# One paced sequence for the mixers of all four chunks, with the last two feed-forwards standing alone

## The chip, the cores and the metric

The kernel runs on one core of one Trainium2 chip. The metric is the device time of one execution in microseconds (us). The engines in the text are PE (TensorE: matrix products; PEld is its loading of the stationary operand), DVE (VectorE), ACT (ScalarE), POOL (GpSimd, which here issues DMAs) and SP (which issues DMAs too).

## The reference

One decoder block works on 2048 positions of width 1024, all in float32:

```
h   = rms_norm(x) * (1 + sc1) + sh1
proj = h @ w_in                       # 3088 columns: gq gk gv gr glr aq ak av
y_gla = gated linear attention, 4 heads, chunks of 64, state carried along the sequence
y_att = dilated attention, 8 heads, (window, dilation) = (128,1), (512,4), (2048,16), merged per position
x   = x + g1 * (concat(y_gla, y_att) @ w_out)
h   = rms_norm(x) * (1 + sc2) + sh2
u   = causal depthwise conv of width 3 over (h @ w_up)     # 2 x 2816 columns
x   = x + g2 * ((silu(u_gate) * u_val) @ w_down)
```

The six vectors sh1, sc1, g1, sh2, sc2, g2 come from one product of the condition with a weight of 1024 x 6144.

## The kernel before

The sequence is cut into four chunks of 512 positions (`NCH = 4`, `T = 512`). Each float32 product of weights is made of three passes in a rounded format (`mm3`, lines 306 to 308: high by high, high by low, low by high); a weight block arrives raw (L234), its high part is cut by ACT (L240) and its low part by DVE (L241). These products go to the four PSUM banks of the pool `psg`. The mixers use the four banks of the pool `psa`.

The generators of the program `yield` between steps, and `run` interleaves them:

- `gemm` is the projection of the four chunks with the late part of the condition product beside it: 100 steps of about 24 matmuls. `run` takes 27 of them ahead, so that 73 are left.
- `mix(c)` is the mixers of chunk `c`, 68 steps: two halves of linear attention (`gla`, 14 steps each: DVE lines 690 to 725 prepare and mask, PE L680 makes the scores, L739 to L779 the rest) and four pairs of attention heads (`attn`, 10 steps each: PE L865 and L830 make scores, DVE L836 adds the bias and takes the maximum, ACT L840 the exponentials, PE L897, L921 and L850 the merging factors and transposes, L949 and L954 the products with the values, L969 and DVE L972 the end).
- `outproj(c)` is the output projection, 8 steps, after which comes the second norm's statistic (PE L445, ACT L447 and L448), then a tail of work that was put off (4 or 8 steps), then the normalised input `h2` of the feed-forward (DVE L465, ACT L467, DVE L469).
- `ffn(c)` is the feed-forward: 44 up blocks of 24 matmuls (evacuated by ACT L1028, DVE L1029 to L1045) and five groups of 8 down steps of 12 matmuls (evacuated by DVE L1073); a sixth group is put off as the next chunk's tail.

`beside(a, na, b, nb)` takes `na / nb` steps of `a` after each step of `b`, and what is left of `a` at the end. Before, it is called four times: `mix(0)` beside the 73 steps of `gemm` (68/72, or 0.94 of a step each), and `mix(1)`, `mix(2)`, `mix(3)` beside `outproj(c-1)` and `ffn(c-1)` (96, 100 and 100 steps, at 68/90, 68/86 and 68/90: 0.76 to 0.79). `outproj(3)` and `ffn(3)` come last with nothing beside them.

```
def beside(a, na, b, nb):
    acc = 0.0
    done = object()
    for _ in b:
        acc += na / nb
        while acc >= 1.0:
            acc -= 1.0
            if next(a, done) is done:
                acc = -1e9
    for _ in a:
        pass
```

The order so written is the input of a scheduler that fixes each engine's order when the program is built; each engine then works through its own queue in order.

Of the kernel before, what the change touches and what calls it, by code (L numbers as in the profile page):

```python
# [21 lines left out]
NCH = 4  # L22
# [78 lines left out]
# [14 lines that stand above are left out]
def along(a, na, b, nb):  # L115
# [9 lines that stand above are left out]
        yield  # L125
    for _ in a:
        pass


def chain(*gs):  # L130
    for g in gs:
        yield from g


class K:
# [945 lines left out]
    def run(self):  # L1081
        self.ada_setup()
        self.scratch()
        self.x1, self.h2, self.tail = {}, {}, ()
        self.planned = False
        xs = self.load_x(0)
        acc = None
        for k in range(5):
            acc = self.square(acc, xs[k])
        sqs = [self.tmp.tile([P, T], F32, name="sq", bufs=3) for _ in range(5, KD)]  # L1090
        for sq, x in zip(sqs, xs[5:]):
            self.nc.scalar.activation(sq, x, AF.Square)
        rstd = {0: self.norm_end(acc, more=sqs)}
        h0, ws, done = [], {}, {b: self.pg() for b in FIRST}
        spare = self.at.tile([P, 2048], F32R, name="w0", tag="kt", bufs=2)
        ring = self.at.tile([P, 2048], F32, name="ring", tag="kt", bufs=2)
        for k in range(KD):
            big = [self.at.tile([P, 1024], F32, name="wada", tag="big", bufs=4)]
            pair = [self.gp.tile([P, T], F32, name="wada", tag=t) for t in ("ghi", "glo")] if k < 5 else [ring[:, (k - 5) * 1024:(k - 4) * 1024] if k < 7 else self.at.tile([P, 1024], F32, name="wada", tag="v4", bufs=1)]
            gs = [self.ada(KD + k, big), self.ada(k, pair)]  # L1100
            for g in gs:
                next(g)
            if k < len(FIRST):
                b = FIRST[k]
                ws[b] = self.wblock(self.A["w_ch"][b], KD, P, spare if k == 3 else None)
            for g in gs:
                next(g, None)
            if k == GATE:
                self.gate_ins = self.last
            h0.append(self.norm_mod1(xs[k], k, rstd[0], self.G1, self.mod[:, 0:8]))  # L1110
        for b in FIRST:
            for k in range(KD):
                self.mm3(done[b], ws[b][k:k + 1], h0[k:k + 1], k == 0, True)
        self.consts()

        def src(c):
            def f(k):
                t = self.tmp.tile([P, T], F32, name="sq", bufs=3)
                ld = self.dq.dma_start(t, self.A["xT"][c, k])
                if c == 1:  # L1120
                    self.after(ld)
                return t
            return f

        self.wleft, self.wready, self.wpos = list(self.plan()), [], 0
        self.planned = True
        hs = [h0]

        def begin(c):
            hs.append(self.norm_mod(src(c), rstd[c], self.G1, self.mod[:, 0:8]))  # L1130

        def proj(c):
            yield from self.proj(c, hs.pop(), (lambda: begin(c + 1)) if c < 3 else None, () if c else done)

        def stats(c):

            acc = None
            xs = [src(c)(0)]
            yield
            for k in range(KD):  # L1140
                if k + 1 < KD:
                    xs.append(src(c)(k + 1))
                yield
                acc = self.square(acc, xs[k], xs[k])
            yield
            rstd[c] = self.norm_end(acc, split=True)
            yield

        def ahead(c):

            return along(stats(c), 11, proj(c - 1), 18)

        gemm = along(self.ada_late(), 66, chain(ahead(1), ahead(2), ahead(3), proj(3)), 94)
        for _ in range(27):
            next(gemm)
        beside(self.mix(0), 68, gemm, 72)
        beside(self.mix(1), 68, chain(self.outproj(0), self.ffn(0)), 90)
        beside(self.mix(2), 68, chain(self.outproj(1), self.ffn(1)), 86)
        beside(self.mix(3), 68, chain(self.outproj(2), self.ffn(2)), 90)
        for _ in chain(self.outproj(3), self.ffn(3)):  # L1160
            pass


# [59 lines left out]
```

## Time and profile before

| | |
|---|---|
| time | 2602.16 us, median of 2 runs (2600.97 and 2603.35) |
| profiled execution, first to last instruction | 2603.1 us, 46834 instructions |
| PE busy | 2559.7 us, 18142 matmul records |
| DVE busy | 1930.2 us |
| ACT busy | 1277.7 us |
| POOL busy | 444.4 us |
| mean granted TensorE clock | 0.994 |
| DMA | 405.13 MB, mean 156 GB/s |

The page gives the profiled execution no time of its own beside its span; the longer of the two runs is 0.25 us above that span. A matmul's record lasts until its modelled end, so records of one engine overlap: the rate of PE is read from the starts of its rows, not from its busy share. The stages of the span, by the first row of each: the projection with `mix(0)` from about 205 to 722 us, then three stretches from one feed-forward's first up block to the next, 1237.5, 1740.2 and 2237.2 us, and the last feed-forward alone from there to the end.

### The profile page before, as it was taken

Reading aid. Unit: us, or ns where it says so; the run is one execution under the profiler, and the core shown is the slowest. Engines: PE = TensorE matmul, PEld = TensorE weight load, DVE = VectorE, ACT = ScalarE, POOL = GpSimd, SP = SyncE. Lnnn points to the kernel's source line nnn. Section 1 sums busy time; section 2 is a strip of 40 time slices with the busy share of each in tenths; the row PEclk is TensorE's granted clock in tenths of the full one; section 3 lists DMA queues with packets and bytes.
Section 4 is the critical chain, followed back from the end, with each engine's and each line's share of the span. In section 5 each row is a group of like instructions: output and inputs, shape, how many; then the busy total and the mean of one; then the engine's idle time right before and its main releaser. Section 6 shows DMA issues by size and latency. Waiting matters only on the chain.

```text
span 2603.1 us, 46834 instructions
## 1 busy us (share of the span) xinstructions
PE 2559.7 (98%) x18142; PEld 2104.0 (81%) x18142; DVE 1930.2 (74%) x4091; ACT 1277.7 (49%) x2626; POOL 444.4 (17%) x816
## 2 busy tenths in 40 slices
PE   5999999999999999999999999999999999999999
PEld 4888888788788888887788888878888888788887
DVE  7578877768788777777987777689777775766665
ACT  4566556656454444454545544346445453433332
POOL 1343332313210000012100000310000003100001
PEclk8999999999999999999999999999999999999999
DMA  8766675756633344455334344733443435432322
GB/s 291 242 226 234 211 236 170 239 167 201 230 108 100 123 128 122 127 174 199 123 96 139 117 134 136 252 131 114 129 140 127 143 103 189 150 103 97 96 96 84
DMA packets 164194, 405.13 MB, mean 156 GB/s; under 512 B 19154, under 2 KB 61956, under 8 KB 162692
## 3 DMA queue, kind: packets, MB, share of 16 engines
q0 software_dynamic: 88128, 308.59, 35.5%
q1 hardware_dynamic: 75844, 93.55, 11.6%
q8 instruction: 143, 2.34, 0.4%
q14 instruction: 79, 0.65, 0.1%
HBM read 339.15 MB, written 62.91 MB: 154 GB/s over the span
## 4 chain that ended last, share of the span: by engine, by line
PE 77%; issue 1%; DVE 1%; DMA 1%; ACT 0%; POOL 0%; POOLq 0%; DVEq 0%; ACTq 0%
PE psg L306 22%; PE psg L307 22%; PE psg L308 22%; PE psa L850 2%; PE psa L830 2%; PE psa L954 2%; PE psa L680 1%; PE psa L949 1%; PE psa L865 0%; PE psa L753 0%; PE psa L752 0%; PE psa L969 0%; DMA wada<-in_w_ada_dram 0%; PE psa L757 0%; PE psa L779 0%
## 5 line engine op out<-in xcount | busy, mean ns | idle before, releaser
L306 PE MATMUL psg<-hhi,whi 128*128 128x512 f32 x1992 | 782.0, 396 | 9.2 <-ACT hhi L467 5.3
L307 PE MATMUL psg<-hlo,whi 128*128 128x512 f32 x1992 | 782.9, 394 | 6.7 <-DVE hlo L469 6.5
L308 PE MATMUL psg<-hhi,wlo 128*128 128x512 f32 x1992 | 780.2, 392 | 0.7 <-DVE wlo L241 0.7
L240 ACT CAST whi<-wraw 128x1024 fp32r<-128x1024 f32 (+1 forms) x391 | 410.4, 1051 | 467.4 <-PE psg L307 363.2
L241 DVE TENSOR_TENSOR wlo<-wraw,whi 128x1024 fp32r<-128x1024 f32 (+1 forms) x391 | 478.0, 1223 | 187.2 <-ACT whi L240 181.5
L306 PEld LDWEIGHTS psg<-hhi,whi 128*128 128x128 f32 x1992 | 375.0, 189 | 95.2 <-ACT hhi L467 9.3
L307 PEld LDWEIGHTS psg<-hlo,whi 128*128 128x128 f32 x1992 | 375.3, 188 | 86.7 <-DVE hlo L469 9.6
L308 PEld LDWEIGHTS psg<-hhi,wlo 128*128 128x128 f32 x1992 | 375.5, 188 | 80.6 <-issue 1.7
L306 PE MATMUL psg<-ghi,whi 128*128 128x512 f32 x744 | 295.1, 398 | 0.0
L307 PE MATMUL psg<-glo,whi 128*128 128x512 f32 x744 | 292.1, 393 | 0.5 <-DVE glo L999 0.5
L308 PE MATMUL psg<-ghi,wlo 128*128 128x512 f32 x744 | 291.6, 392 | 0.0
L234 POOL DMA_DIRECT2D wraw<-in_w_up_dram x176 | 93.6, 532 | 982.6 <-DVE wlo L241 850.5
L1073 DVE SCALAR_TENSOR_TENSOR x<-psg,mod,x 128x512 f32<-128x512 f32 x192 | 143.2, 749 | 118.2 <-PE psg L308 115.7
L306 PE MATMUL psg<-whi,hhi 128*128 128x512 f32 (+2 forms) x512 | 172.8, 345 | 8.3 <-ACT stg L523 6.2
L308 PE MATMUL psg<-whi,hlo 128*128 128x512 f32 (+2 forms) x512 | 174.8, 345 | 0.0
L307 PE MATMUL psg<-wlo,hhi 128*128 128x512 f32 (+2 forms) x512 | 174.6, 343 | 0.1
L306 PEld LDWEIGHTS psg<-ghi,whi 128*128 128x128 f32 x744 | 139.5, 188 | 34.0 <-issue 5.3
L307 PEld LDWEIGHTS psg<-glo,whi 128*128 128x128 f32 x744 | 139.8, 188 | 30.0 <-issue 1.9
L308 PEld LDWEIGHTS psg<-ghi,wlo 128*128 128x128 f32 x744 | 139.7, 188 | 29.5 <-issue 0.7
L840 ACT ACTIVATE big<-big,nm 128x256 f32<-128x256 f32 (+1 forms) x256 | 122.4, 480 | 33.6 <-DVE nm L855 33.4
L1028 ACT ACTIVATE y<-psg,tables_sb 128x512 f32<-128x512 f32 x176 | 136.1, 776 | 4.5 <-PE psg L308 3.2
L1029 DVE SCALAR_TENSOR_TENSOR y<-psg,tables_sb,y 128x511 f32<-128x511 f32 x176 | 130.7, 743 | 3.7 <-ACT y L1028 3.6
(253 smaller groups left out, 3621.9 us busy)
## 6 DMA issues: line engine op xcount, KB each, us to landing
wraw<-in_w_up_dram POOLq DMA_DIRECT2D x176, 512.0 KB, 3.6
wraw<-in_w_down_dram POOLq DMA_DIRECT2D x88, 512.0 KB, 3.6
wraw<-in_w_ch_dram POOLq DMA_DIRECT2D x44, 512.0 KB, 4.3
v<-v SPq DMA_DIRECT2D x68, 256.0 KB, 5.6
wada<-in_w_ada_dram POOLq DMA_DIRECT2D x64, 256.0 KB, 4.8
wraw<-in_w_tokw_dram POOLq DMA_DIRECT2D x32, 512.0 KB, 4.2
wraw<-in_w_out_dram POOLq DMA_DIRECT2D x32, 512.0 KB, 4.7
sq<-in_xT_dram POOLq DMA_DIRECT2D x48, 256.0 KB, 4.9
```

The costliest lines, as they stand in the source:

```text
L234: self.dq.dma_start(raw[:, :n], src)
L240: nc.scalar.copy(hi[:, :n], raw[:, :n])
L241: nc.vector.tensor_tensor(lo[:, :n], raw[:, :n], hi[:, :n].bitcast(F32), op=ALU.subtract)
L306: nc.tensor.matmul(ps, wh, hh, start=first and k == 0, stop=False, skip_group_check=shared)
L307: nc.tensor.matmul(ps, wh, hl, start=False, stop=False, skip_group_check=shared)
L308: self.lastmm = nc.tensor.matmul(ps, wl, hh, start=False, stop=k == n - 1, skip_group_check=shared)
L830: nc.tensor.matmul(at(i, hh, z), q[H[hh], i * P:(i + 1) * P], key(H[hh], i, z), start=True, stop=True, skip_group_check=True)
L840: nc.scalar.activation(t[:, lo:hi], t[:, lo:hi], AF.Exp, bias=nm[:, hh, g, i:i + 1], scale=2.0 ** -(h + 1), accum_out=dn[:, hh, g, i:i + 1])
L850: nc.tensor.transpose(ps[:n, i * P:(i + 1) * P], part(S[hh], i), self.C("id"))
L1028: nc.scalar.activation(y, ps, AF.Identity, bias=self.cb[:, b:b + 1], scale=self.cw[:, 2, b:b + 1])
L1029: nc.vector.scalar_tensor_tensor(y[:, 1:], ps[:, :T - 1], self.cw[:, 1, b:b + 1], y[:, 1:], op0=ALU.mult, op1=ALU.add)
L1073: nc.vector.scalar_tensor_tensor(x1, ps, self.mod[:, 40 + cb:41 + cb], x1, op0=ALU.mult, op1=ALU.add)
```

## The change

The four calls and the lone end become one call and a longer lone end. All 272 mixer steps run in one sequence, at 272/243 = 1.12 steps after each step of the chain `gemm`, `outproj(0)`, `ffn(0)`, `outproj(1)`, `ffn(1)` (73 + 96 + 100 = 269 steps). `outproj(2)`, `ffn(2)`, `outproj(3)`, `ffn(3)` then have nothing beside them. The order of the products of weights among themselves is the same, and so is the order of the mixers' steps among themselves; no instruction of either is added or removed.

```
-        beside(self.mix(0), 68, gemm, 72)
-        beside(self.mix(1), 68, chain(self.outproj(0), self.ffn(0)), 90)
-        beside(self.mix(2), 68, chain(self.outproj(1), self.ffn(1)), 86)
-        beside(self.mix(3), 68, chain(self.outproj(2), self.ffn(2)), 90)
-        for _ in chain(self.outproj(3), self.ffn(3)):
+        beside(chain(*(self.mix(c) for c in range(NCH))), 272, chain(gemm, self.outproj(0), self.ffn(0), self.outproj(1), self.ffn(1)), 243)
+        for _ in chain(self.outproj(2), self.ffn(2), self.outproj(3), self.ffn(3)):
             pass
```

On PE, this is the place behind `outproj(2)`, where the statistic of the norm (L445) is made and the put-off down steps of chunk 1 follow. Before:

```order
L307 MATMUL psg<-glo,whi 128x512
L308 MATMUL psg<-ghi,wlo 128x512
L445 MATMUL psa<-rstd,ones 128x512
L680 MATMUL psa<-pt 32x32 x64
L306 MATMUL psg<-ghi,whi 128x512
L307 MATMUL psg<-glo,whi 128x512
```

And PE at the same place in the changed kernel:

```order
L307 MATMUL psg<-glo,whi 128x512
L308 MATMUL psg<-ghi,wlo 128x512
L445 MATMUL psa<-rstd,ones 128x512
L306 MATMUL psg<-ghi,whi 128x512
L307 MATMUL psg<-glo,whi 128x512
```

The 64 score matmuls of `mix(3)` (L680) that stood there are gone to an earlier place: the last mixer matmul of the program (L969) stands behind 7851 of the 9792 `psg` matmuls before, and behind 5878 in the changed kernel.

On DVE, this is the start of the second half of linear attention of chunk 2 (`mix(2)`), with the work of the feed-forward around it. L663 to L704 are the mixers', L1029 to L1073 the feed-forward's, L241 the low part of a weight. Before:

```order
L183 COPY stage<-psa 128x512
L241 TENSOR_TENSOR wlo<-wraw,whi 128x1024
L663 COPY kt<-psa 128x512
L1041 SCALAR_TENSOR_TENSOR y_13467<-th,y_13467 128x512
L1029 SCALAR_TENSOR_TENSOR y_13558<-psg,tables_sb,y_13558 128x511
L1032 SCALAR_TENSOR_TENSOR y_13558<-halo,tables_sb,y_13558 128x1
L700 TENSOR_TENSOR pt<-kt 128x512
L1030 SCALAR_TENSOR_TENSOR y_13558<-psg,tables_sb,y_13558 128x510
L1045 TENSOR_TENSOR glo<-y_13467,ghi 128x512
L1033 SCALAR_TENSOR_TENSOR y_13558<-halo,tables_sb,y_13558 128x2
L1040 SCALAR_TENSOR_TENSOR th<-th,y_13513 128x512
```

And DVE at the same step of `mix(2)` in the changed kernel:

```order
L183 COPY stage<-psa 128x512
L663 COPY kt<-psa 128x512
L700 TENSOR_TENSOR pt<-kt 128x512
L1073 SCALAR_TENSOR_TENSOR x<-psg,mod,x 128x512
L241 TENSOR_TENSOR wlo<-wraw,whi 128x1024
L703 TENSOR_TENSOR pt<-kt,pt 128x512
L700 TENSOR_TENSOR pt<-kt 128x512
L704 TENSOR_TENSOR pt<-kt,pt 128x512
L1073 SCALAR_TENSOR_TENSOR x<-psg,mod,x 128x512
L703 TENSOR_TENSOR pt<-kt,pt 128x512
L700 TENSOR_TENSOR pt<-kt 128x512
L704 TENSOR_TENSOR pt<-kt,pt 128x512
```

The step stood among up blocks and now stands among down steps, and the rows of the mixers stand closer together: one or two operations for the feed-forward stand between three of theirs, where before three or four stood between two of theirs.

## Prediction

> **What bounds the kernel now.** I read the page first, then the table by stages, then PE's waits, then the starts of single matmuls.
>
> ```profile
> PE 2559.7 (98%) x18142; PEld 2104.0 (81%) x18142; DVE 1930.2 (74%) x4091; ACT 1277.7 (49%) x2626; POOL 444.4 (17%) x816
> PE   5999999999999999999999999999999999999999
> PE 77%; issue 1%; DVE 1%; DMA 1%; ACT 0%; POOL 0%; POOLq 0%; DVEq 0%; ACTq 0%
> ```
>
> PE is busy in every slice but the first, and the chain that ended last runs through PE for 77%, with 1% each for DVE and DMA. Since matmul records overlap, "busy" alone would hide small gaps; the starts settle it. In the last feed-forward, which has no mixer beside it:
>
> ```profile
> 2300.69 0.39 PE L307 MATMUL psg<-hlo,whi 128*128 128x512 f32 x1
> 2300.92 0.39 PE L308 MATMUL psg<-hhi,wlo 128*128 128x512 f32 x1
> ```
>
> One matmul of 512 columns per 0.23 us (0.227 over longer stretches). The stages, with the columns length, then busy time of PE, PEld, DVE, ACT and POOL, granted clock, DMA share, GB/s:
>
> ```profile
> 205.00:722.00 517.00, 512.26 (x4245) 428.23 (x4236) 398.08 (x918) 312.67 (x673) 158.20 (x282) 1.00 0.63 208
> 1237.50:1740.20 502.70, 498.61 (x3868) 407.20 (x3866) 387.31 (x892) 243.79 (x551) 60.54 (x113) 1.00 0.44 142
> 1740.20:2237.20 497.00, 494.69 (x3507) 403.75 (x3507) 372.27 (x855) 236.78 (x529) 60.97 (x114) 1.00 0.43 137
> 2190.00:2237.20 47.20, 44.99 (x195) 35.93 (x193) 28.40 (x36) 21.01 (x27) 9.12 (x17) 1.00 0.46 152
> 2237.20:2603.00 365.80, 361.17 (x1584) 298.25 (x1584) 236.80 (x369) 126.57 (x156) 38.98 (x73) 0.99 0.29 97
> ```
>
> A feed-forward alone takes 365.8 us, its output projection about 47.2: 413. With a mixer sequence beside it the period is 497, so a mixer sequence costs 84 us of PE time (497 less 413), in line and not hidden. The same subtraction on DVE: 372.3 less (236.8 + 28.4) is 107 us per sequence. PE has no room to give, so four sequences cost about four times 84 us wherever they stand. A reordering can only win or lose at the seams.
>
> **The change part by part.** No instruction is added or removed; 272 mixer steps move earlier. The sum is made against the profiled span of 2603.1 us, 0.9 above the median of the runs shown.
>
> *Seams between products of weights and mixers.* Each visit of PE to the mixers costs something at both ends:
>
> ```profile
> 1199.09 0.39 PE L308 MATMUL psg<-hhi,wlo 128*128 128x512 f32 x1
> 1199.41 0.29 PE L680 MATMUL psa<-kt 64*32 64x32 f32 x11
> ...
> 1199.91 0.50 PE L306 MATMUL psg<-hhi,whi 128*128 128x512 f32 x1
> 1200.25 0.40 PE L307 MATMUL psg<-hlo,whi 128*128 128x512 f32 x1
> ...
> 1009.13 0.39 PE L306 MATMUL psg<-ghi,whi 128*128 128x512 f32 x1
> 1009.36 0.60 PE L850 MATMUL psa<-consts_sb,big 128*128 128x128 f32 x4
> 1009.71 0.47 PE L307 MATMUL psg<-glo,whi 128*128 128x512 f32 x1
> 1010.02 0.39 PE L308 MATMUL psg<-ghi,wlo 128*128 128x512 f32 x1
> ```
>
> The last matmul before L680 holds PE 0.32 us (1199.09 to 1199.41) in place of 0.23, the first behind it 0.34: 0.2 us per visit. Around the transposes of L850 only the way out costs: 0.31 in place of 0.23, so 0.08. The built order has 334 visits before and 316 after, 18 fewer. At 0.15, between the two rows, that is **-2.7 us**; the ends are 18 times 0.08 and 18 times 0.2, or -1.4 and -3.6.
>
> *The boundary of chunk 2 loses its cover.* Behind an output projection PE works through the put-off steps and then waits for the normalised input. First with mixers beside it (chunk 2), then bare (chunk 3):
>
> ```profile
> 1738.13 0.39 PE L308 MATMUL psg<-ghi,wlo 128*128 128x512 f32 x1
> 1740.16 0.47 PE L306 MATMUL psg<-hhi,whi 128*128 128x512 f32 x1 [1.64 <-DVE x L1073]
> 1740.72 0.51 PE L307 MATMUL psg<-hlo,whi 128*128 128x512 f32 x1
> 1741.07 0.40 PE L308 MATMUL psg<-hhi,wlo 128*128 128x512 f32 x1
> ...
> 2235.33 0.39 PE L308 MATMUL psg<-ghi,wlo 128*128 128x512 f32 x1
> 2237.18 0.47 PE L306 MATMUL psg<-hhi,whi 128*128 128x512 f32 x1 [1.46 <-ACT hhi L467]
> 2237.75 0.50 PE L307 MATMUL psg<-hlo,whi 128*128 128x512 f32 x1
> ...
> 2239.28 0.63 PE L308 MATMUL psg<-hhi,wlo 128*128 128x512 f32 x1
> 2239.70 0.63 PE L306 MATMUL psg<-hhi,whi 128*128 128x512 f32 x1
> ```
>
> The covered boundary loses 2.03 less 0.23, 0.56 less 0.23 and 0.35 less 0.23: 2.3 us. The bare one loses 1.85 less 0.23 and 0.57 less 0.23, about 2.0 us, and then shows starts 0.42 us apart (2239.28 to 2239.70), which the covered one does not. Seven of those and a few smaller delays make up about 2 us more. One boundary changes from covered to bare: **+2 us**, between 0 (the wait itself is no longer than the covered one's) and +4 (the wait of 2.0 us comes twice).
>
> The Trainium skill, "TensorE: Matmul & The Clock Gate", Part 1 ("The HAM clock gate"), says that the array falls to half its clock after an idle window of about 3.4 us and comes back after a busy one as long. The doubled spacing here is such a clock, but the wait ahead of it was 1.46 us, under the window, and the covered boundary with 1.64 us kept its clock. By that rule the term would lose its clock part and be near 0; by the row it is +2.
>
> *The mixers' closer pace.* A step comes every 0.89 steps of the weights' products (243/272) in place of 1.06 beside the projection and 1.26 to 1.32 beside the feed-forwards. Whether PE then waits for the mixers' DVE and ACT work is the unknown. What PE waits for in `psa` now, the long wait at the start apart:
>
> ```profile
> PE psa L779 <- DVE pt L773: 0.9, 1, 0.9
> PE psa L680 <- DVE stage L972: 0.6, 1, 0.6
> PE psa L969 <- DVE pt L934: 0.3, 1, 0.3
> PE psa L662 <- DVE ll L657: 0.2, 1, 0.2
> ```
>
> That is 2.0 us in the whole span, though `mix(0)` already ran at 0.94 of a step. DVE's load: 82 of the 272 steps (73 times 1.12) now fall beside the projection, 190 (2.8 sequences) beside two feed-forwards. There PE has 2 times 413 plus 2.8 times 84, or 1061 us, and DVE 2 times 265 plus 2.8 times 107, or 830: 78%, against 75% in the row of chunk 2. Beside the projection DVE gets 398 plus 14 steps of 1.6 us (107/68), or 420 of 534 us: 79% against 77%. The cover is thin but there. The nearest row says 2 us of waits for 272 steps; a pace 1.2 to 1.5 times as close I value at **+3 us**. Bounds: -2 (those waits go) and +24, if each of the 12 pairs of heads beside the feed-forwards lost the 2.0 us that the worst four losses make up together.
>
> *The start of `outproj(0)`* no longer follows the end of `mix(0)` directly: that sequence ends at step 61 of 73, so its last stores are a dozen steps old when they are read back. The L680 wait of 0.6 us and the boundary's small ones may go: **-1 us**, 0 to -2. The end of the program (`outproj(3)` and `ffn(3)`) is as it was: 0.
>
> Sum: -2.7 + 2 + 3 - 1 = +1.3, or 2604.4 us; I say **2604**. The bounds add to 2595.5 (-3.6, 0, -2, -2) and 2629.7 (-1.4, +4, +24, 0).
>
> **The rivals.**
>
> *The chain inside a pair of heads becomes the bound; slower.* Ends of two pairs now:
>
> ```profile
> 1022.67 1.06 DVE L972 TENSOR_TENSOR stage<-psa,stage 128x512 f32<-128x512 f32 x1 [3.69 <-ACT stage L971]
> 1095.78 1.07 DVE L972 TENSOR_TENSOR stage<-psa,stage 128x512 f32<-128x512 f32 x1 [0.76 <-ACT stage L971]
> ```
>
> A pair took 73 us. Ten steps at the new pace are 8.9 steps of the feed-forward at 413/98 = 4.2 us and 10/68 of 84 us: 50 us. If scores, maxima, exponentials, merging factors and transposes need longer than that one after another, PE, which works in order, stands still at L897, L921 or L850 with products of weights queued behind it. It decides from 52/12 = 4.3 us per pair on, which is 2% of the time; at 6 us per pair the time is 2603 + 72 = 2675. For it: in the built order the fourth pair of chunk 2 ends some 100 `psg` matmuls (22 us) behind its pace, so the sequence is already held by its chain there. Against it: that delay was put into the order by moving mixers back, and PE fills it with products of weights; and at L897, L921 and L850, which already stand a few matmuls behind what they need, PE waits for nothing now.
>
> *DVE binds in the dense stretches of linear attention; a little slower.* In the rows of the change three mixer operations stand for each one or two of the feed-forward's. Six halves stand beside feed-forwards; if each holds PE up by 5 us, a quarter of a group of 8 down steps (22 us), the time is 2603 + 30 = 2633. Against it: the free banks of `psg` give 4 times 12 times 0.227, or 11 us of grace. The Trainium skill, "SBUF — State Buffer", section "Who interferes with whom", adds that VectorE in a two-port mode shuts GpSimd out, so that weights issued from POOL would come late too; no run here shows such a lock.
>
> *More than 2% faster.* All seams together are 316 visits that remain and at most 334 times 0.2, or 67 us, of which 18 go. To win 52 us, PE's waits inside the mixers would have to be large and hidden; the four rows above say 2 us. Time if every seam loss of the 18 visits and all waits above go: 2596.
>
> **Chances.** Forecast (2592 to 2618): 0.78. DVE in the dense stretches (2618 to 2655): 0.13. The chain of a pair (above 2655): 0.07. Much faster: 0.02. The range runs from 2592 to 2632, which holds a bit over 0.8. Faster by over 2% 0.02, within 2% 0.91, slower by over 2% 0.07; 2% is about what a measurement of this kernel can tell from no change.
>
> **What would show it.** The seams: PE's total of `psa` waits, and 0.3 us starts around L680, fewer by 18 pairs. The boundary: behind the third L445 after the start, starts 0.42 us apart as behind the fourth. The pace: PE's waits for L897, L921, L850 or L680, each a few us at most in sum; pairs of heads 50 us apart at L972; DVE near 78% from the first output projection to the end of the mixers, then 65%. The prediction is wrong if PE's busy slices fall to 9 tenths or less in the middle of the span, or if the stage with mixers ends later than four times 84 us of mixers allow.

## The result, and the profile after

The changed kernel takes **2634.27 us** (median of 2 runs, 2632.76 to 2635.78) against 2602.16: a ratio of 1.0124, with a 95% interval of 1.0094 to 1.0153. It is slower, and its median lies 2 us above the predicted range and 30 us above the predicted time; the interval, about 2627 to 2642 us, still reaches into the range. The profiled execution spans 2631.0 us, 27.9 us more than before.

The first lines of its page hardly differ from those of before. PE is as busy in every slice, and DVE has the same work; only its slices in the last third show that the mixers end earlier. What has changed is the chain that ended last: it now follows PE for 45% only, and the load of `kw` stands among its lines. (The listed shares add up to 47%, so this chain leaves half of the span untold, and the drop from 77% is no measure of lost time.)

```profile
PE 2573.8 (98%) x18142; PEld 2116.4 (80%) x18142; DVE 1933.7 (73%) x4091; ACT 1276.6 (49%) x2624; POOL 445.2 (17%) x816
PE   5999999999999999999999999999999999999999
DVE  7678977768787769877679877865766665766665
PE 45%; DVE 1%; DMA 1%; issue 0%; ACT 0%; SPq 0%; POOL 0%; POOLq 0%
```

The stages of the changed kernel (length, busy time of PE, PEld, DVE, ACT and POOL, clock, DMA share, GB/s): first the two stretches with mixers, from 722 us (in the output projection of chunk 0) to about the feed-forward of chunk 1 and from there to about that of chunk 2, then the two that stand alone.

```profile
722.00:1331.00 609.00, 605.24 (x5186) 489.66 (x5185) 472.12 (x1184) 315.98 (x796) 63.84 (x119) 1.00 0.44 143
1331.00:1852.00 521.00, 512.34 (x4041) 420.82 (x4039) 397.96 (x924) 250.30 (x570) 59.89 (x112) 0.99 0.42 139
1852.00:2263.00 411.00, 408.69 (x1796) 336.60 (x1795) 266.51 (x407) 160.87 (x239) 63.68 (x119) 1.00 0.36 123
2263.00:2631.00 368.00, 361.70 (x1587) 298.46 (x1585) 238.66 (x372) 128.54 (x159) 38.98 (x73) 0.99 0.29 98
```

DVE is at 472.12 of 609 and 397.96 of 521 us, 78% and 76%, and then at 65%: as forecast, and not the bound. PE's waits tell more (engine, tile and line, the one waited for: us in total, times, longest):

```profile
PE psg L306 <- ACT hhi L467: 12.6, 5, 4.4
PE psa L830 <- DMA kw<-k: 6.4, 8, 1.2
PE psa L865 <- DMA qf<-q: 2.9, 1, 2.9
PE psa L830 <- DVE md L836: 2.0, 2, 1.7
```

Waits for `kw`, `qf` and `md` are not in the list of before at all, and the wait for `hhi` is larger (12.6 against 5.3 us).

**Where the time went.** I took every time from one matmul's start to the next one's on PE and summed it by the line of the first. The sum grows by 28.2 us: 13.9 at the score matmuls L830 (65.2 to 79.1), 7.1 at L865, behind which the waits for `kw` stand (14.0 to 21.1), 4.2 in the products of weights, 2.6 at L501, 1.7 at L969, and 1.3 less in all others. Three places make most of it.

*The load of `kw`.* `kt`, `kw` and `v16` share two buffers, so the next pair's `kw` can only be loaded when L949 of this pair has read `v16`. Before, on PE and then on SP's queue:

```profile
1495.67 3.71 PE L954 MATMUL psa<-big,v 128*64 128x128 f32 x64
1518.34 1.13 PE L830 MATMUL psa<-kw,qf 64*128 64x256 f32 x8
...
1495.80 0.53 SPq L806 DMA_DIRECT2D kw<-k  x1
```

After:

```profile
902.08 3.71 PE L954 MATMUL psa<-big,v 128*64 128x128 f32 x64
906.31 0.86 PE L865 MATMUL psa<-kt,qf 64*32 64x64 f32 x64
908.14 1.10 PE L830 MATMUL psa<-kw,qf 64*128 64x256 f32 x4 [0.97 <-DMA kw<-k]
...
902.21 0.53 SPq L806 DMA_DIRECT2D kw<-k  x1
```

L954 starts when the last L949 has been issued, and the load follows 0.13 us later in both. Before, PE wants `kw` 22.5 us after that. After, it comes for `kw` within 6 us, and the load takes about 5.9 (902.21 to 908.14). From the last L949 of a pair to the first L830 of the next one, within a chunk, there were 13 to 29 us before (one of 5.0 in chunk 0, whose `kw` is smaller); after, eight of the twelve are 5.3 to 6.7 us.

*Scores of one head alone.* The scores of two heads use the two halves of the array. Before, eight records of both heads, and after, four records of one head:

```profile
1106.54 1.14 PE L830 MATMUL psa<-kw,qf 64*128 64x256 f32 x8
1107.60 0.50 PE L306 MATMUL psg<-ghi,whi 128*128 128x512 f32 x1
...
917.32 1.13 PE L830 MATMUL psa<-kw,qn 64*128 64x256 f32 x4
918.38 0.50 PE L308 MATMUL psg<-hhi,wlo 128*128 128x512 f32 x1
```

Both take 1.06 us: one head alone costs as much as the two together, so 0.5 us per run is lost. There were 8 runs of four records before and there are 25 now; in the traces 4 of the 8 and 23 of the 25 take 1.03 to 1.06 us, and 19 times 0.53 is about 10 of the 13.9 us at L830. The Trainium skill, "TensorEngine Tiling (Array Packing)", section "Available Configurations", lists this split of the array into two tiles of 64 rows; the two rows show both halves at work at once, and what half of it left idle costs.

*The norm of chunk 1.* On ACT, first in the kernel before and then in the changed kernel, and below it PE in the changed kernel:

```profile
1232.17 0.69 ACT L447 ACTIVATE rstd<-psa,eps 128x512 f32<-128x512 f32 x1
1234.17 0.63 ACT L448 ACTIVATE rstd<-rstd 128x512 f32<-128x512 f32 x1
...
1330.78 0.69 ACT L447 ACTIVATE rstd<-psa,eps 128x512 f32<-128x512 f32 x1
1331.49 1.28 ACT L840 ACT_TABLE_LOAD   x1
1332.78 0.51 ACT L840 ACTIVATE big<-big,nm 128x256 f32<-128x256 f32 x1
...
1336.24 0.61 ACT L448 ACTIVATE rstd<-rstd 128x512 f32<-128x512 f32 x1
...
1334.20 0.39 PE L308 MATMUL psg<-ghi,wlo 128*128 128x512 f32 x1
1338.95 1.22 PE L306 MATMUL psg<-hhi,whi 128*128 128x512 f32 x2 [4.36 <-ACT hhi L467]
...
1342.43 0.63 PE L307 MATMUL psg<-hlo,whi 128*128 128x512 f32 x1
1342.86 0.63 PE L308 MATMUL psg<-hhi,wlo 128*128 128x512 f32 x1
```

Seven exponentials of a mixer stand between the two steps of the norm's root, which before followed each other. PE waits 4.36 us and then has starts 0.43 us apart; the granted clock is 0.50 from 1338.4 to 1345.2 us. In the 30 us behind the last put-off product, the starts of weights' products lose 6.7 us against 0.227 us each; before it was 2.3.

*The clock.* The mean granted clock is 0.994 in the profile before and 0.992 in this one. An estimate from it: one less the clock, times the span, is 16 us before and 21 after, so up to 5 of the 28 us are stretches at half clock, which the sums above already hold. The share is larger in some runs below: by the same estimate up to 24 of the 53 us that the span of the first run is longer (clock 0.985), and up to 35 of the 80 us at the closest pace (0.981). It is an upper end, because a low clock costs nothing while PE waits, and no run here changes the clock by itself.

### The profile page after: what moved, and what is told of

Same layout as the page of the kernel before. It is cut to its first block, busy times and chain, and to the rows that moved or that the text cites. A ratio compares the mean times of both kernels' runs of the same rounds, so it can differ in the third digit from the quotient of the medians.

```text
span 2631.0 us, 46869 instructions
## 1 busy us (share of the span) xinstructions
PE 2573.8 (98%) x18142; PEld 2116.4 (80%) x18142; DVE 1933.7 (73%) x4091; ACT 1276.6 (49%) x2624; POOL 445.2 (17%) x816
## 5 line engine op out<-in xcount | busy, mean ns | idle before, releaser
L306 PE MATMUL psg<-hhi,whi 128*128 128x512 f32 x1992 | 779.5, 395 | 14.7 <-ACT hhi L467 12.6
L241 DVE TENSOR_TENSOR wlo<-wraw,whi 128x1024 fp32r<-128x1024 f32 (+1 forms) x391 | 478.2, 1223 | 186.9 <-ACT whi L240 181.5
L1073 DVE SCALAR_TENSOR_TENSOR x<-psg,mod,x 128x512 f32<-128x512 f32 x192 | 143.4, 748 | 116.5 <-PE psg L308 116.1
L1029 DVE SCALAR_TENSOR_TENSOR y<-psg,tables_sb,y 128x511 f32<-128x511 f32 x176 | 130.9, 744 | 3.1 <-ACT y L1028 3.0
```

What stands on the lines that cost most here:

```text
L241: nc.vector.tensor_tensor(lo[:, :n], raw[:, :n], hi[:, :n].bitcast(F32), op=ALU.subtract)
L306: nc.tensor.matmul(ps, wh, hh, start=first and k == 0, stop=False, skip_group_check=shared)
L1029: nc.vector.scalar_tensor_tensor(y[:, 1:], ps[:, :T - 1], self.cw[:, 1, b:b + 1], y[:, 1:], op0=ALU.mult, op1=ALU.add)
L1073: nc.vector.scalar_tensor_tensor(x1, ps, self.mod[:, 40 + cb:41 + cb], x1, op0=ALU.mult, op1=ALU.add)
```

## The experiments

**Theory 1:** the closer pace costs, inside the mixers: late `kw`, runs of one head, exponentials in the norm. **Theory 2:** something else does: the chaining of chunks, or a PE that would lose the same elsewhere whatever is mended. The texts of the first four runs were written when the parts of theory 1 were still taken for rivals of one another; the theories that they name are those parts. Ratios are against the kernel before on the same chip. In kernels with added lines, a line stands a little lower than in the changed kernel (L835 for L830, and L856 or L861 where the tie of score matmuls is added).

**First attempts at the changed kernel: two misses, a control and a hit.** The first ties the first score matmul of each pair of banks to the release of both heads' banks:

```
+                    if hh == 0 and i % 2 == 0 and both[i + 1] is not None:
+                        self.tie(mm, both[i + 1])
```

> The changed kernel, with the first score matmul of each pair of heads (L830) made to wait until the banks of both heads are free, so that the two heads' matmuls, which use the two halves of the array, are again issued side by side (runs of one head alone: 25 in the order of the changed kernel, 8 before, 11 here). Theory (the loss is in PE's own order: score matmuls of one head alone, which take 1.03 us for what takes 0.52 us side by side): L830 falls from 79 us to about 70 us and the time by 7 to 9 us, to about 2626 us. Rival (DVE and ACT are too busy in the dense stretches and PE waits for them): the time stays at 2634 us or rises, since PE now waits for one more bank.

Measured: 2655.34 us, ratio 1.0198 (1.0183 to 1.0213). Slower, not faster, as its rival said. L830 fell from 79.1 to 75.0 us, but PE waits elsewhere, longer than before the tie:

```profile
PE psa L856 <- DMA kw<-k: 13.5, 7, 2.9
PE psa L925 <- DVE xm L147: 9.9, 1, 9.9
```

The second takes no mixer step beside the put-off steps behind `outproj(1)`:

```
+        HOLD[0] = c == 1
         yield from self.tail
+        HOLD[0] = False
```

> The changed kernel, with no mixer step taken beside the 8 put-off down steps behind the output projection of chunk 1; the sequence ends 8 steps later. Theory (seven exponentials of the mixers stand on ACT between the logarithm and the exponential of the norm's statistic and hold up the normalised input by 4.8 us): the boundary of chunk 1 loses about 4 us, as the bare ones do, in place of 8, and the time falls by 3 to 5 us, to about 2630 us. Rival (it is load over the whole stage, not this place): no difference, 2634 us.

Measured: 2637.25 us, 1.0131 (1.0116 to 1.0146). A miss: the exponentials had been written into the order before the hold began (they still stand behind L447 on ACT), and PE's gap was still 4.78 us.

The third is a control for the fourth, which gives `kw` a buffer of its own; the room comes from the weights' blocks.

```
-        self.whi = pool("whi", 4)
-        self.wlo = pool("wlo", 4)
+        self.whi = pool("whi", 3)
+        self.wlo = pool("wlo", 3)
...
-    def weights(self, name, *idx, ahead=3):
+    def weights(self, name, *idx, ahead=2):
```

> Control for the next run: the changed kernel with three slots in place of four for the high and the low part of the weights and one block less of look-ahead, which makes room in SBUF. Both theories: 2634 us if the weights' look-ahead is ample, up to 2645 us if not.

```
-        kw = self.at.tile([P, 13 * P], F32, name="kw", tag="kt", bufs=2)
+        kw = self.at.tile([P, 13 * P], F32, name="kw", bufs=1)
```

> As the control, with a buffer of its own for the keys of the two short windows (kw), so that their load no longer waits until the products with the values of the pair before (L949) have freed a buffer; PE's order is the control's, row for row. Theory (PE waits at L865 and L830 for loads that are issued only then, 11 us in the changed kernel): 8 to 11 us below the control, and the waits of PE L830 for the load of kw are gone. Rival (DVE and ACT are the hold-up): the same as the control within 3 us, with the waits turned into waits for DVE.

Measured: 2645.77 us (1.0163, 1.0148 to 1.0178) and 2637.52 us (1.0128, 1.0111 to 1.0145). The control lies just above its upper end of 2645. The waits for `kw`, 10.6 us in the third, are gone in the fourth, and so are 8.3 us of the time, with the same order on PE. Late `kw` costs most of what its waits show; the smaller ring of weights, about 11 us dearer than the changed kernel, took that back.

**The pace alone.** The projection keeps `mix(0)` as before; `mix(1)` to `mix(3)` stand in one sequence beside the three pairs of output projection and feed-forward, at four paces (266, 220, 182 or 150 for `nb`):

```
         beside(self.mix(0), 68, gemm, 72)
-        ...                    # the three calls of before for mix(1) to mix(3)
+        beside(chain(*(self.mix(c) for c in range(1, NCH))), 204, chain(*(g for c in range(3) for g in (self.outproj(c), self.ffn(c)))), nb)
         for _ in chain(self.outproj(3), self.ffn(3)):
```

> Mixers of chunks 1 to 3 in one chained sequence beside the three pairs of output projection and feed-forward, but at the pace of before (204 steps beside 266, 0.77 of a step each); the projection keeps mix(0) at 68/72 as before. Theory 1, the closer pace inside the mixers is what costs: nothing is closer here, so 2600 to 2607 us, within 0.2% of before, and score matmuls of one head alone stay at 8 runs. Theory 2, chaining the sequences over the chunk boundaries costs by itself (a mixer step of the next chunk standing in another chunk's boundary): 2612 us or more.

> The same with 204 steps beside 220, 0.93 of a step each. Theory 1: 21 runs of score matmuls of one head in place of 8 (13 times about 0.5 us, 7 us) and some late loads of kw: 2608 to 2616 us. Theory 2: as the run at 0.77.

> The same with 204 steps beside 182, 1.12 of a step each, the pace of the changed kernel, with the projection left as before. Theory 1: the feed-forward part of the loss, 20 to 28 us: 2622 to 2632 us, waits for the load of kw at L830 6 us or more. Theory 2: as the run at 0.77. If the loss sat beside the projection instead (mix(0) at 1.12 in place of 0.94), this run is near 2605.

> The same with 204 steps beside 150, 1.36 of a step each. Theory 1: the loss keeps growing, to 2640 us or more, with longer waits of PE at L830 and the transposes, and DVE over 90% where the mixers run. Theory 2: as the run at 0.77.

| mixer steps per step | time (us) | ratio (95%) | waits for `kw` | runs of one head | L830, starts (us) |
|---|---|---|---|---|---|
| before, 0.76 to 0.79 | 2604.87 | | none | 8 | 65.2 |
| 0.77 | 2602.48 | 0.9992 (0.9984 to 1.0001) | none | 8 | 66.3 |
| 0.93 | 2630.15 | 1.0097 (1.0083 to 1.0111) | 9.2 | 21 | 77.5 |
| 1.12 | 2629.38 | 1.0098 (1.0085 to 1.0112) | 9.5 | 29 | 84.1 |
| 1.36 | 2681.56 | 1.0291 (1.0277 to 1.0305) | 18.3 | 24 | 89.4 |

The chaining costs nothing: theory 2 in that form falls. The pace costs, and beside the feed-forwards most of all: at 1.12 this run loses 24.5 us and the changed kernel 32.1, each against the kernel before as it was measured beside it. My number at 0.93 was 14 us too low: the loss does not grow evenly but appears between 0.77 and 0.93, where the time from L949 to the next L830, in chunks 1 to 3, falls from 16 us or more to 7 to 10 in most pairs. From 0.93 to 1.12 the time does not move. In the last row PE also waits at the merging factors and transposes, which the prediction had feared at the pace of the change; DVE was busy for 76% from 722 to 1720 us there, not over 90% as expected:

```profile
PE psa L830 <- DMA kw<-k: 18.3, 7, 7.7
PE psa L897 <- DVE xm L894: 8.0, 1, 8.0
PE psa L921 <- DVE xm L913: 2.5, 2, 1.5
```

**Each part by itself.** In the changed kernel, the products of `v16` and the DVE step behind them directly follow the transposes that they need, so that the buffer comes free two steps earlier:

```
+        O16 = self.pa()        # the products of v16 (L949), moved up unchanged
+        ...
+        acc = weigh(O16, 0)
         yield                  # two steps of transposes follow, then L954
```

> The changed kernel with the products of v16 (L949, and the DVE step L934 behind them) two steps earlier in the pair of heads, directly behind the transposes that they need, so that the buffer that the next pair's kw takes is free earlier. No memory is added. Theory 1 (the late load of kw costs by itself): PE's waits for kw at L830 fall from 6.4 us to under 2, and in the built order the runs of score matmuls of one head fall from 25 to 16; 6.4 + 9 times 0.5 us, or about 10 us less: 2622 to 2628 us. Rival (at this pace PE only waits at the next place in its queue): 2632 us or more, with the time back at L830 behind DVE, or at L865, L897, L850.

Measured: 2624.24 us (1.0083, 1.0069 to 1.0097), 10 us less than the changed kernel, as theory 1 said; the two intervals overlap by a little. One wait for `kw` is left:

```profile
PE psa L830 <- DMA kw<-k: 1.1, 1, 1.1
```

From L949 to the next L830 there are now 16 us or more in 11 of the 12 pairs. The second half of the theory's sum is not borne out as it was meant: nine runs of one head fewer are 4.8 us, but three pairs now stop inside their scores for a bank, about 1.1 us each (shown below), and L830 falls by 4.1 us in all, 2.0 of them the waits for `md`. The edit also moves the DVE step that frees a bank of `psa`, so it is not the load alone that it changes; the run in which `kw` has a buffer of its own is the cleaner price of the load, 8.3 us.

The next holds the mixers back from the fifth step of `outproj(1)` on, early enough that no exponential stands in the norm:

```
+            HOLD[0] = c == 1 and cb >= 4
             yield
```

> The changed kernel in which no mixer step is taken from the fifth step of outproj(1) until its put-off down steps are done, so that no exponentials of the mixers are waiting on ACT when the norm's L447 and L448 come. Theory: the gap of 4.75 us of PE behind the put-off steps of chunk 1 falls to 2 us or less, and the time by 2 to 4 us, to 2630 to 2632 us. Rival: the exponentials that stood there stand elsewhere and the gap stays over 4 us, as in the run that only held the put-off steps: 2634 us or more.

Measured: 2643.21 us (1.0156, 1.0142 to 1.0170): a miss in the time and a hit in the trace. PE's longest gap at the norm is 1.05 us in place of 4.75. But the waits for `kw` rose to 10.6 us, the longest 3.1, and the mean granted clock fell to 0.989:

```profile
PE psa L835 <- DMA kw<-k: 10.6, 6, 3.1
```

So this part can be judged only where `kw` is not late. That is the next but one, which has both edits:

> Both of the first two edits in the changed kernel: v16's products early, and no mixer step from the fifth step of outproj(1) to the end of its put-off steps. Theory 1: the gains add, about 12 us: 2620 to 2626 us; what is left over before is the one-head runs (22 in the built order against 8, 7 us), and the boundaries of chunks 0 and 2 (4 us). Rival: no better than the better one of the two alone.

Measured: 2619.71 us (1.0066, 1.0054 to 1.0079), a further 4.5 us less, though the intervals of the two runs overlap. In it, ACT does the two steps of the norm one behind the other, and PE waits 0.81 us:

```profile
1310.12 0.69 ACT L452 ACTIVATE rstd<-psa,eps 128x512 f32<-128x512 f32 x1
1311.77 1.28 ACT L453 ACT_TABLE_LOAD   x1
1313.06 0.63 ACT L453 ACTIVATE rstd<-rstd 128x512 f32<-128x512 f32 x1
...
1316.61 0.47 PE L311 MATMUL psg<-hhi,whi 128*128 128x512 f32 x1 [0.81 <-ACT hhi L472]
```

The price of a head alone was put into the kernel before, at its own pace: in chunk 2 each head's scores are a step of their own.

```
+            for n in range(8):
+                i, hh = (n % 4, n // 4) if c == 2 else (n // 2, n % 2)
...
+                if c == 2 and n == 3:
+                    yield
```

> The kernel before, with the scores of chunk 2 (L830) written head by head in two steps with products of weights between them: in the built order 8 runs of one head's 4 matmuls and 8 of the other's replace runs in which both heads alternate. Nothing else moves closer; the 76 steps of mix(2) stand beside the same 86. Theory 1 (one head alone uses half the array and takes as long as both together): 8 groups by about 1.9 us more, or 15 us, and a little for 8 more visits: 2616 to 2622 us, with L830 16 us over its 65.2. Rival (a run of one head costs no more per matmul, and its longer spacing only shows a wait for banks): 2602 to 2608 us.

Measured: 2622.05 us (1.0075, 1.0062 to 1.0087), 19 us more, at the upper end of what theory 1 said. The starts at L830 add up to 14.2 us more, and eight records of one head take 1.92 us where eight of both took 1.06:

```profile
1517.13 1.99 PE L830 MATMUL psa<-kw,qf 64*128 64x256 f32 x8
1519.05 0.50 PE L306 MATMUL psg<-hhi,whi 128*128 128x512 f32 x1
```

**What is left.** With both edits, 17 us over before remain, and L830 has 12 of them (77.2 against 65.2). In the trace 18 runs of one head take 1.06 us, against 4 before, which is about 7 us; and three score runs stop after two records for a bank that L977 (L972 of the changed kernel) of the pair before releases, and take 2.16 us in place of 1.06, which is 3 more:

```profile
1650.85 0.70 PE L835 MATMUL psa<-kw,qf 64*128 64x256 f32 x2
1651.95 1.13 PE L835 MATMUL psa<-kw,qf 64*128 64x256 f32 x6 [0.41 <-DVE stage L977]
```

The tie of the first attempt was tried again where `kw` and the norm are in time, and in the kernel before:

> The run with both edits (v16's products early, no mixer step around the norm of chunk 1), and besides the first score matmul of each pair of banks tied to the release of both heads' banks, so that the built order has 10 runs of one head alone in place of 20. Theory 1 (what is left over before, 17 us, is mostly one-head runs, and the tie was bad before only because kw and the norm of chunk 1 were late behind it): 10 runs by 0.5 us, 5 us less, 2612 to 2617 us. Rival (a PE that is held for both banks loses as much at the next places of its queue, whatever else is late): 2622 us or more.

> The kernel before with the same tie of the score matmuls to both heads' banks: 4 runs of one head alone in place of 8. Theory 1: 4 times 0.5 us, 2 us less, 2598 to 2603 us. Rival: the tie itself holds PE at the slow pace too, 2608 us or more.

Measured: 2625.13 us (1.0077, 1.0064 to 1.0091) and 2605.61 us (1.0003, 0.9994 to 1.0012). At the slow pace the tie is harmless. At the close pace the time is in the rival's range: PE issues fewer runs of one head alone, but it waits for the other's bank, and L830 only falls to 75.9.

```profile
1321.88 1.13 PE L861 MATMUL psa<-kw,qf 64*128 64x256 f32 x4
1325.81 2.07 PE L861 MATMUL psa<-kw,qf 64*128 64x256 f32 x4 [2.80 <-DVE stage L152]
```

Last, the banks themselves: five for `psa` and three for `psg`, in the kernel before, in the changed kernel, with both edits, and at the pace of 0.77.

```
-        self.psg = pool("psg", 4, space=PSUM)
-        self.psa = pool("psa", 4, space=PSUM)
+        self.psg = pool("psg", 3, space=PSUM)
+        self.psa = pool("psa", 5, space=PSUM)
```

> The kernel before with five banks of PSUM for the mixers (psa) and three for the products of weights (psg), in place of four and four. In the built order no run of one head alone is left (8 before) and PE visits the mixers 290 times in place of 334. Theory 1 (the banks of psa decide both): 4 us less for the runs and 44 times 0.145, or 6 us, for the visits: 2590 to 2596 us. Rival (three banks of psg make PE wait for DVE and ACT to empty them): 2603 us or more, with new waits at the first matmul of a psg bank.

> The changed kernel with five banks of psa and three of psg: 10 runs of one head alone in place of 25 and 258 visits in place of 316, at the same pace. Theory 1: 15 times 0.5 us and 58 times 0.145, or 16 us less: 2614 to 2622 us, with the waits for kw as they were. Rival (three banks of psg make PE wait, and more so where DVE is denser): 2632 us or more.

> The run with both edits (v16's products early, no mixer step around the norm of chunk 1) with five banks of psa and three of psg: 11 runs of one head alone in place of 20 and 282 visits in place of 297. Theory 1: 5 us and 2 us less, 2610 to 2615 us; with that the loss of the close pace would be told but for about 8 us. Rival: 2620 us or more, the waits of PE only change their place, as with the tie.

> The mixers of chunks 1 to 3 in one sequence at the pace of before (204 steps beside 266) with five banks of psa and three of psg: 2 to 4 runs of one head alone in place of 8 and 271 visits in place of 313. Theory 1: 3 us and 42 times 0.145, or 6 us, less than that run's 2602.5: 2591 to 2597 us, faster than both kernels. Rival: PE waits for banks of psg, 2603 us or more.

Measured: 2649.01 (1.0170, 1.0154 to 1.0185), 2660.26 (1.0215, 1.0200 to 1.0230), 2658.25 (1.0211, 1.0189 to 1.0233) and 2642.37 us (1.0139, 1.0122 to 1.0156). Four misses: the times are the rival's, and with three banks the starts of the products of weights take 13 to 31 us more. Part of that is the clock: it is 0.986 to 0.988 in these four profiles, by the estimate above up to 19 of the 41 us in the kernel before, and which wait sets it off is not shown. In that run the largest new wait is for DVE in the linear attention (L680, 11.0 us), so the banks of `psg` are not shown to be the whole cause either. What theory 1 said of L830 is still in the traces, in three of four: the starts at L830 fall from 65.2 to 60.3, from 79.1 to 71.0 and from 66.3 to 62.1; with both edits they rise from 77.2 to 78.6. In the changed kernel with five banks, the largest wait of PE is for a feed-forward's bank:

```profile
PE psg L306 <- DVE x L1073: 12.8, 4, 4.0
```

No version beat the kernel before; one sequence at its pace equals it.

## Why the prediction was wrong

**The step that failed is the term for the closer pace.** It said +3, between -2 and +24; it was about +28 (27.9 less the other three, which come out near nothing together). The mechanism that I named for it, PE waiting for the mixers' DVE and ACT work, with thin cover, is a small part as a wait (2.0 us for `md`). I valued it by PE's waits at the old pace (2.0 us), and a load that comes 7 us before its reader, or more, does not show in such a list at all. Measured in its place: about 8 us for late `kw` (8.3 when it had its own buffer), about 10 us for the runs of one head alone (19 more at that price), and about 4.4 us for the exponentials in the norm of chunk 1 (6.7 less 2.3). That is 22 to 23 of the 28 us. The edits that mend the first and the last gave 14.5 us together and left 17, of which L830 has 12. The upper bound came near by chance: it counted pairs of heads, not the chain of `kw`. Since even the sum of all upper bounds, 2629.7 us, lay below the result, the bounds were too narrow too. The prediction also took 2% as about what a measurement of this kernel can tell; the intervals here reach 0.1 to 0.3% to either side.

**Seams: nearly right.** Against 0.227 us for a product of 512 columns, and in proportion for fewer, the 316 visits lose 48.2 us at both ends where 334 lost 47.0. Without the single wait of 2.9 us for `qf`, which falls on one of them, that is 45.3, so -1.7 where -2.7 was said, inside the ends of -1.4 and -3.6.

**The bare boundary of chunk 2: too high.** The wait came as forecast, but no starts 0.42 us apart:

```profile
1856.01 0.39 PE L308 MATMUL psg<-ghi,wlo 128*128 128x512 f32 x1
1857.86 0.47 PE L306 MATMUL psg<-hhi,whi 128*128 128x512 f32 x1 [1.46 <-ACT hhi L467]
1858.43 0.50 PE L307 MATMUL psg<-hlo,whi 128*128 128x512 f32 x1
1858.77 0.39 PE L308 MATMUL psg<-hhi,wlo 128*128 128x512 f32 x1
1858.99 0.63 PE L306 MATMUL psg<-hhi,whi 128*128 128x512 f32 x2
```

The granted clock stays at 1.00 from 1858 to 1862 us. Over 30 us this boundary loses 2.2 us, against 2.8 for the covered one before: -0.6 in place of +2. By the rule of the Trainium skill that the prediction weighed ("TensorE: Matmul & The Clock Gate", Part 1) the term was near 0, and here the trace agrees. It does not agree for chunk 3, where the same wait of 1.46 us is again followed by slow starts, 0.43 us apart, at a granted clock of 0.50. There the loss over 30 us is 3.7 us, so the rule held in one of the two bare cases, and that it held at chunk 2 may be luck.

**The start of `outproj(0)`: wrong in sign.** It was to gain 1 us. The L680 wait of 0.6 us is gone, but PE waits 1.80 us for `ghi`, and slow starts follow at a granted clock of 0.50:

```profile
682.21 0.97 PE L306 MATMUL psg<-ghi,whi 128*128 128x512 f32 x3 [1.80 <-ACT ghi L998]
683.96 0.63 PE L308 MATMUL psg<-ghi,wlo 128*128 128x512 f32 x1
684.38 0.63 PE L306 MATMUL psg<-ghi,whi 128*128 128x512 f32 x1
```

**The rivals.** The chain inside a pair did not become the bound at this pace: PE waits nowhere at L897, L921 or L850, and pairs come 52 to 62 us apart in chunks 1 to 3, but for one (50 was said). It does at 1.36. DVE's dense stretches did not bind either; its load was forecast rightly. The time came out where that rival put it (2618 to 2655), for other reasons. The rival that was missing is a DMA: a load that shares its buffers with the work of the pair before, and that nobody waited for as long as the pairs stood apart.

**What stays open.** That the runs of one head come from banks of `psa` that come free one by one rests on the built order, on the stops for L977's bank and on three of the four runs with five banks; no run took them away at the close pace without another loss, so their 10 us are read from the starts and from the run that wrote them into the kernel before. Scores of both heads in one bank might keep them together; that was not tried. Not told apart, either, are the other 5 of the last 17 us, and how much of each loss is the wait itself and how much the half clock that can follow it.

## What to carry to other kernels

Before work is moved closer together, list for each load the time from the release of its buffer to its first reader, and compare it with the time that the load takes: a list of waits shows nothing of a margin that is about to be used up. Where two half-array products are meant to run side by side, look in the built order for runs of one of them alone. A mended stall only pays where the next thing in the queue is not late as well, so judge it together with its neighbour.

## What was not expected of the hardware

One half of the array alone takes as long as both (1.06 us for four records as for eight). The same wait of 1.46 us left the clock alone at the bare boundary of chunk 2 and was followed by starts 0.43 us apart at that of chunk 3, in both kernels; waits of 1.80 and 4.36 us were followed by such starts, and one of 1.64 us before was not. In these two profiles the granted clock then stands at 0.50 for 3.4 us, or for 6.8 behind the longest of these waits. The change of tables on ACT between the two functions of the norm took 1.28 us, with the next operation 0.01 us behind it.
